# Moving weight buffers by 192 bytes: fourteen units to distance 0 from the activations, streamed weights to distance 192

## The chip, the cores and the metric

The kernel runs on one core of one Trainium2 chip. The metric is the device time of one execution in microseconds (us), lower is better. Five engines work side by side: TensorE (in the profile PE for matmuls, PEld for weight loads), VectorE (DVE), ScalarE (ACT), GpSimd (POOL) and SyncE (SP), which here only issues DMAs. A matmul takes two operands from the on-chip memory SBUF: the stationary one, called weights, is loaded by a weight load; the other is streamed past it. Results go to PSUM.

## What is computed

A trunk of two layers on 256 tokens of width 1024, in float32. Each layer is an FFN, a mixer, a second FFN and a gated input embedding, all residual:

```
for i in range(DEPTH):                                   # DEPTH = 2
    h = h + 0.5 * swiglu(rms_norm(h, ffn1_norm[i]), ffn1_w_gate[i], ffn1_w_up[i], ffn1_w_down[i])
    hn = rms_norm(h, mix_norm[i])
    if i % N_MIXERS == 0:  m = rglru_mixer(hn, ...)      # layer 0: recurrent mixer
    else:                  m = pool_mixer(hn, ...)       # layer 1: causal pooling
    h = h + m
    h = h + 0.5 * swiglu(rms_norm(h, ffn2_norm[i]), ffn2_w_gate[i], ffn2_w_up[i], ffn2_w_down[i])
    gate = jax.nn.sigmoid(rms_norm(h, ple_norm[i]) @ ple_w_gate[i])
    h = h + gate * (p[i] @ ple_w_proj[i])
return rms_norm(h, final_norm)

def swiglu(x, w_gate, w_up, w_down):
    return (jax.nn.silu(x @ w_gate) * (x @ w_up)) @ w_down
```

An FFN is 1024 wide outside and 2816 inside, so it holds most of the weights; there are four of them.

## The kernel before

All weights come as 328 units of 128x1024 floats, in the order in which they are used (`ORDER`). A unit is loaded by one DMA from SyncE into a `raw` tile, and then `split` makes of it a high part (a copy on ScalarE rounded to fp32r) and a low part (the rest, by a subtraction on VectorE), side by side in one `hl` tile of 2 x 1024 floats. Activations are split in the same way (`x`, `hid`, and `yr` with `ytp`). A product is then three fp32r matmuls (`mm3`): high weights with high activations, high weights with low activations, low weights with high activations. A unit feeds 24 such matmuls, of 128x128 weights and 256 streamed columns each. The units of the recurrent gates (`lru_gates`) are used unsplit, straight from `raw`. `unit` runs seven loads and four splits ahead of use.

Mostly the weights are stationary and activations stream. There are three exceptions: in `proj` (result `pp`) the transposed input embedding `ple_in`, which is one of the units, streams against the units `ple_proj`; in the pooling mixer the unit `pool_w` streams against activations (result `v`), and the units `pool_op` stream against `vhl` (result `po`).

The order of work in an FFN: the first two column pairs of gate and up are projected in two halves of the inner dimension (`project_all`), so that the work can begin before all of `x` is there. In the second half, `rstd_tokens` adds one-off matmuls for the sums of squares (`ss`, four of one column, each recorded as two) and `rstd_spread` two that spread the result over the partitions (`spread`, recorded as four). In three of the four FFNs, and in the RG-LRU layer, the spread falls in the middle of the second job of that half, and in the first FFN in the middle of the third. In the first gate projection it falls in the middle of the second job, in the last one in the middle of the first. Then the down projection of an earlier pair and gate and up of the next pair take turns up to pair 10 (results `acc`, `gate`, `up`), and nothing but these matmuls runs on TensorE. In the second FFN `proj` stands in the middle, ahead of pair 5.

Where the tiles lie follows from the pools, which are set up in this order:

```
rawp = ctx.enter_context(tc.tile_pool(name="raw", bufs=5))
hlp = ctx.enter_context(tc.tile_pool(name="hl", bufs=6))
gap = ctx.enter_context(tc.tile_pool(name="gap", bufs=1))     # one tile of 48 floats, 192 bytes
hp = ctx.enter_context(tc.tile_pool(name="h", bufs=6))
xp = ctx.enter_context(tc.tile_pool(name="x", bufs=7))
```

A `raw` tile takes 4096 bytes of each partition, an `hl` tile 8192, an `h` tile 2048, an `x` or `hid` tile 4096. Operands of matmuls begin at multiples of 512 bytes within their tile. Distance below means: start address of the streamed operand minus start address of the weights, in bytes modulo 512. The gap tile makes it 192 wherever activations stream against units; in `pp` it is 0, in `v` 320 (the gap counted the other way).

Of the kernel before, what the change touches and what calls it, by code (L numbers as in the profile page):

```python
# [10 lines left out]
F32R = mybir.dt.float32r  # L11
# [4 lines left out]
P = 128  # L16
# [12 lines left out]
U = 1024  # L29
# [17 lines left out]
APART = 48  # L47
# [24 lines left out]
def stream_order():  # L72

    order = []

    def halves(*keys):

        return [k + (kh,) for kh in range(2) for k in keys]

    def ffn(l, which, middle=()):  # L80
        def gu(p):
            return [(which, l, m, p, kh) for m in ("gate", "up") for kh in range(2)]

        def down(p):
            return [(which, l, "down", p, f) for f in range(2)]

        out = halves(*[(which, l, m, p) for p in range(2) for m in ("gate", "up")]) + down(0)
        for p in range(2, NF2):
            out += (list(middle) if p == NF2 // 2 else []) + gu(p) + down(p - 1)
        return out + down(NF2 - 1)  # L90

    def ple(l):
        return halves(*[("ple_gate", l, j) for j in range(NP_)])

    def proj(l):
        return [("ple_in", l)] + [("ple_proj", l, k) for k in range(2)]

    def pairs(kind, *ps):
        return [(kind, p, kh) for p in ps for kh in range(2)]

    def gates(hf):
        return [("lru_gates", hf, b) for b in range(-(-len(GATE_BLOCKS[hf]) // 8))]

    order += ffn(0, "ffn1")
    order += halves(*[(f"lru_{s[0]}", int(s[1])) for s in LRU_FIRST])
    for s in LRU_STEPS:
        kind, i = s[0], int(s[1])
        order += gates(i) if kind == "g" else pairs(f"lru_{kind}", i) if kind in "xb" else []
    order += [("lru_out", k) for k in range(NR)]
    order += ffn(0, "ffn2", proj(0)) + ple(0)  # L110
    order += ffn(1, "ffn1")
    order += [("pool_w", k) for k in range(2)] + proj(1) + [("pool_op", k) for k in range(2)]
    order += ffn(1, "ffn2") + ple(1)
    return order


ORDER = stream_order()


POOL_COLS = ((0, P + 16), (P, S))  # L120
# [3 lines left out]
def width(key):  # L124
    if key[0] == "lru_gates":
        return min(8, len(GATE_BLOCKS[key[1]]) - 8 * key[2]) * P
    if key[0] == "ple_in":
        return 2 * S
    if key[0] == "pool_op":
        return 4 * (POOL_COLS[key[1]][1] - POOL_COLS[key[1]][0])  # L130
    return U


def pack_units(a):
# [8 lines left out]
    for g, win in enumerate(WINDOWS):  # L143
        for t in range(S):
            lo = max(0, t + 1 - win)
            op[g, lo:t + 1, t] = np.float32(1.0) / np.float32(t + 1 - lo)
            op[g, t, t] = np.float32(1.0) / np.float32(t + 1 - lo) - np.float32(1.0)
    w = np.zeros((len(ORDER), P, U), np.float32)

    def rows(m):  # L150
        return m.reshape(-1, P, m.shape[1]).transpose(1, 0, 2).reshape(P, -1)

    for n, u in enumerate(ORDER):
        kind = u[0]
# [58 lines left out]
def trunk(ctx: ExitStack, tc: tile.TileContext, xT, vec, w, out):  # L213
# [4 lines left out]
    hlp = ctx.enter_context(tc.tile_pool(name="hl", bufs=6))  # L218
# [43 lines left out]
    def load(n, parts=1):  # L262
        whole = ORDER[n][0] == "lru_gates"
        raw = (box["gates"] if whole else rawp).tile([P, U], F32, tag="raw", name=f"raw{n}")
        step = width(ORDER[n]) // parts
        for i in range(parts):
            c = slice(i * step, (i + 1) * step)
            nc.sync.dma_start(raw[:, c], w[n, :, c])
        (units if whole else raws)[ORDER[n] if whole else n] = raw

    def split(n, parts=1):
        if n not in raws:
            return
        raw = raws.pop(n)
        hl = hlp.tile([P, 2, U], F32R, tag="hl", name=f"hl{n}")
        step = width(ORDER[n]) // parts
        for i in range(parts):
            c = slice(i * step, (i + 1) * step)
            nc.scalar.activation(hl[:, 0, c], raw[:, c], AF.Copy)  # L279
            nc.vector.tensor_tensor(hl[:, 1, c], raw[:, c], hl[:, 0, c].bitcast(F32), op=ALU.subtract)  # L280
        units[ORDER[n]] = hl

    def unit(*key):
        n = state["used"]
        assert ORDER[n] == key, (ORDER[n], key)
        for what, do, ahead in (("loaded", load, LOADS_AHEAD), ("split", split, SPLITS_AHEAD)):
            while state[what] < min(n + ahead + 1, len(ORDER)):
                do(state[what])
                state[what] += 1
        state["used"] = n + 1  # L290
        return units.pop(key)
# [546 lines left out]
    load_x(0)  # L838
    load(0, 2)
    split(0, 4)  # L840
    load_x(1)
    load(1, 2)
    split(1, 4)
    load(2)
    load(3)
# [39 lines left out]
```

## Time and profile before

| | |
|---|---|
| timed runs | 961.84, 961.54, 958.0 us; median 961.54 |
| profiled execution | 957.91 us, of which the span is 956.0 |
| granted TensorE clock, mean over the span | 0.994 |
| busy: TensorE, VectorE, ScalarE, GpSimd | 98%, 68%, 51%, 6% |
| read from memory | 171.37 MB, 180 GB/s over the span |

The share of TensorE's busy time says that a matmul is under way nearly always; a matmul's record lasts longer than its turn, since the next starts while it drains. How fast they follow each other is therefore read from the number of matmuls in a stretch, and not from the busy share. In the chain of waits, a piece is a run of instructions of one group that follow each other, with its start, its length and its count. Stages in the profile: first FFN up to 189 us, RG-LRU layer up to 298, second FFN up to 488, gate projection up to 512, third FFN up to 703, pooling up to 727, fourth FFN up to 915, gate projection and final norm up to the end.

### The profile page before, as it was taken

How to read it: one execution, taken by the hardware profiler on the slowest of the kernel's cores; microseconds unless marked ns; L12 is line 12 of the kernel's file. 1: busy time of each engine (PE TensorE's matmuls, PEld its weight loads, DVE VectorE, ACT ScalarE, POOL GpSimd, SP SyncE). 2: the span in 40 equal slices, each digit the busy share in tenths (PEclk: the TensorE clock that was granted, in tenths of full speed). 3: DMA queues.
4: the chain of work that ended last, by engine and by line, in shares of the span. 5: the costliest groups of instructions: out<-in, count | busy, mean ns of one | idle time of the engine just before them, and what ended most of it. 6: DMA issues, size and time to landing. Idle time of an engine off the chain costs nothing.

```text
span 956.0 us, 18714 instructions
## 1 busy us (share of the span) xinstructions
PE 937.9 (98%) x7888; PEld 929.7 (97%) x7888; DVE 651.4 (68%) x853; ACT 491.3 (51%) x634; POOL 55.6 (6%) x50
## 2 busy tenths in 40 slices
PE   9999999999999999999998999999989999999997
PEld 9999999999999999999998999999989999999996
DVE  7965565697797655665689755655579765556685
ACT  7544444558775444544457444444458544444443
POOL 1000000023201000000021000000011000000020
PEclk9999999999999999999999999999999999999999
DMA  8866666455445665665634665655534755656611
GB/s 300 288 218 203 195 197 196 159 176 182 133 155 163 210 185 165 219 208 178 207 120 169 218 197 179 193 184 179 184 110 131 250 195 170 205 178 187 188 45 45
DMA packets 49188, 173.63 MB, mean 182 GB/s; under 512 B 5584, under 2 KB 6224, under 8 KB 49104
## 3 DMA queue, kind: packets, MB, share of 16 engines
q1 hardware_dynamic: 48960, 172.29, 55.6%
q8 instruction: 61, 1.00, 0.4%
q14 instruction: 23, 0.19, 0.1%
q10 hardware_dynamic: 144, 0.15, 0.1%
HBM read 171.37 MB, written 1.05 MB: 180 GB/s over the span
## 4 chain that ended last, share of the span: by engine, by line
PE 64%; issue 21%; DVE 11%; ACT 3%; DMA 0%; POOL 0%; DVEq 0%; ACTq 0%; POOLq 0%
PE up0ffn L301 13%; PE gate0ffn L301 13%; PE acc0ffn L301 12%; PE up1ffn L301 6%; PE gate1ffn L301 6%; PE acc1ffn L301 6%; DVE hl L280 3%; DVE x L328 2%; PE x L301 2%; PE accl L301 1%; PE pp L301 1%; PE ri L301 1%; ACT hl L279 1%; PE xb L301 1%; DVE t L517 1%
## 5 line engine op out<-in xcount | busy, mean ns | idle before, releaser
L280 DVE TENSOR_TENSOR hl<-raw,hl 128x1024 fp32r<-128x1024 f32 (+1 forms) x326 | 385.2, 1199 | 228.1 <-ACT hl L279 228.0
L279 ACT ACTIVATE hl<-raw 128x1024 fp32r<-128x1024 f32 (+1 forms) x326 | 332.3, 1036 | 384.2 <-issue 93.0
L301 PE MATMUL gate1ffn<-x,hl 128*128 128x256 f32 x1056 | 130.1, 281 | 3.0 <-DVE x L328 2.4
L301 PEld LDWEIGHTS gate1ffn<-x,hl 128*128 128x128 f32 x1056 | 126.5, 189 | 4.0 <-DVE x L328 3.2
L301 PE MATMUL up1ffn<-x,hl 128*128 128x256 f32 x1056 | 129.5, 281 | 0.0
L301 PE MATMUL acc1ffn<-hid,hl 128*128 128x256 f32 x1056 | 127.6, 281 | 0.0
L301 PE MATMUL gate0ffn<-x,hl 128*128 128x256 f32 x1056 | 126.7, 278 | 0.2
L301 PEld LDWEIGHTS up1ffn<-x,hl 128*128 128x128 f32 x1056 | 126.4, 189 | 0.0
L301 PEld LDWEIGHTS acc1ffn<-hid,hl 128*128 128x128 f32 x1056 | 125.8, 189 | 0.0
L301 PE MATMUL up0ffn<-x,hl 128*128 128x256 f32 x1056 | 125.4, 277 | 0.0
L301 PE MATMUL acc0ffn<-hid,hl 128*128 128x256 f32 x1056 | 124.2, 277 | 0.0
L301 PEld LDWEIGHTS gate0ffn<-x,hl 128*128 128x128 f32 x1056 | 123.3, 188 | 0.8 <-DVE x L328 0.3
L301 PEld LDWEIGHTS up0ffn<-x,hl 128*128 128x128 f32 x1056 | 122.8, 188 | 0.0
L301 PEld LDWEIGHTS acc0ffn<-hid,hl 128*128 128x128 f32 x1056 | 122.1, 188 | 0.3 <-ACT hid L473 0.2
L341 POOL TENSOR_TENSOR sacc<-sq,sq 128x512 f32<-128x512 f32 x9 | 14.9, 1655 | 819.3 <-ACT sq L336 645.8
L328 DVE SCALAR_TENSOR_TENSOR x<-h,vt,x 128x256 fp32r<-128x256 f32 x64 | 48.6, 799 | 6.8 <-ACT x L327 6.8
L301 PE MATMUL ple<-x,hl 128*128 128x256 f32 x384 | 45.6, 278 | 0.2 <-DVE x L328 0.2
L301 PEld LDWEIGHTS ple<-x,hl 128*128 128x128 f32 x384 | 44.4, 188 | 0.5 <-DVE x L328 0.4
L473 ACT ACTIVATE hid<-gs 128x512 fp32r<-128x512 f32 x44 | 27.8, 633 | 17.0 <-DVE gs L471 17.0
L471 DVE TENSOR_TENSOR gs<-th,gs 128x512 f32<-128x512 f32 x44 | 30.4, 692 | 1.5
L327 ACT ACTIVATE x<-h,vt 128x256 fp32r<-128x256 f32 x64 | 28.5, 496 | 5.8 <-DMA vt<-vec 2.5
L474 DVE TENSOR_TENSOR hid<-gs,hid 128x512 fp32r<-128x512 f32 x44 | 30.1, 684 | 0.0
(134 smaller groups left out, 686.4 us busy)
## 6 DMA issues: line engine op xcount, KB each, us to landing
raw<-w SPq DMA_DIRECT2D x320, 512.0 KB, 4.2
raw<-w SPq DMA_DIRECT2D x7, 256.0 KB, 4.5
h<-xT SPq DMA_DIRECT2D x4, 256.0 KB, 6.1
out<-hg SPq DMA_DIRECT2D x3, 256.0 KB, 2.8
raw<-w SPq DMA_DIRECT2D x1, 288.0 KB, 2.6
raw<-w SPq DMA_DIRECT2D x2, 128.0 KB, 5.0
out<-hg SPq DMA_DIRECT2D x2, 128.0 KB, 2.0
vt<-vec ACTq DMA_DIRECT2D x1, 148.0 KB, 4.4
```

The lines of the kernel that those rows point to most:

```text
L279: nc.scalar.activation(hl[:, 0, c], raw[:, c], AF.Copy)
L280: nc.vector.tensor_tensor(hl[:, 1, c], raw[:, c], hl[:, 0, c].bitcast(F32), op=ALU.subtract)
L301: nc.tensor.matmul(o, lhsT, rhs, start=self.first, stop=self.left == 0, skip_group_check=True)
L327: nc.scalar.activation(xt[:, 0, c], h[:, c], AF.Copy, scale=g)
L328: nc.vector.scalar_tensor_tensor(xt[:, 1, c], h[:, c], g, xt[:, 0, c].bitcast(F32), op0=ALU.mult, op1=ALU.subtract)
L341: nc.gpsimd.tensor_tensor(acc, self.acc, sq, op=ALU.add)
L471: nc.vector.tensor_tensor(gs, th, gs, op=ALU.mult)
L473: nc.scalar.activation(hid[:, 0], gs, AF.Copy)
L474: nc.vector.tensor_tensor(hid[:, 1], gs, hid[:, 0].bitcast(F32), op=ALU.subtract)
L517: nc.vector.tensor_tensor(t, accs[j].ps, wide(rq), op=ALU.mult)
```

## The change

The `hl` tile gets 128 floats more (2176 floats, 8704 bytes, a multiple of 512), and a unit's parts begin at an offset in it: 48 floats (192 bytes) for the units in `LEVEL` and for `ple_in`, 96 floats for `pool_w`, 0 for all others. The units in `LEVEL` then stand at distance 0 to the activations; `pp` and `v` come to distance 192. In every FFN two units are in `LEVEL`: the first whole one after the spread (`gate` of pair 1, in the first FFN `up` of pair 1, second half), and the first half of `gate` of pair 6. The other six are in the RG-LRU layer (`lru_x` 2 and 3, `lru_b` 3, `lru_out` 1) and one in each gate projection. The order of instructions on every engine, and what each waits for, is as before.

```
+LEVEL = {(f"ffn{i}", l, "up" if (i, l) == (1, 0) else "gate", 1, 1) for i in (1, 2) for l in range(2)}
+LEVEL |= {(f"ffn{i}", l, "gate", 6, 0) for i in (1, 2) for l in range(2)}
+LEVEL |= {("lru_x", 2, 1), ("lru_x", 3, 0), ("lru_b", 3, 0), ("lru_out", 1), ("ple_gate", 0, 2, 1), ("ple_gate", 1, 1, 1)}
+assert LEVEL <= set(ORDER)
+
+OFFSET = {"ple_in": APART, "pool_w": 2 * APART}
...
         raw = raws.pop(n)
-        hl = hlp.tile([P, 2, U], F32R, tag="hl", name=f"hl{n}")
+        at = APART if ORDER[n] in LEVEL else OFFSET.get(ORDER[n][0], 0)
+        hl = hlp.tile([P, 2 * U + P], F32R, tag="hl", name=f"hl{n}")[:, at:at + 2 * U].rearrange("p (v u) -> p v u", v=2)
```

## Rows read from the trace of the kernel before

**Rows 1.** The page, busy us, share of the span, instructions.
```profile
PE 937.9 (98%) x7888; PEld 929.7 (97%) x7888; DVE 651.4 (68%) x853; ACT 491.3 (51%) x634; POOL 55.6 (6%) x50
```
**Rows 2.** Waits of TensorE: waited for, us in total, times, longest.
```profile
PE v L301 <- DVE x L328: 2.7, 4, 0.8
PE gate1ffn L301 <- DVE x L328: 2.4, 4, 0.8
PE spread L385 <- DVE dg L384: 1.7, 1, 1.7
PE accl L301 <- DVE ytp L700: 1.5, 1, 1.5
...
```
**Rows 3.** Chain of waits, second FFN, 366 to 400 us: start, length, piece.
```profile
373.44 5.65 PE acc0ffn L301 x48
379.09 5.76 PE pp L301 x48
384.85 5.47 PE gate0ffn L301 x48
390.32 5.44 PE up0ffn L301 x48
```
**Rows 4.** Windows: length, then busy (count) by engine, clock, DMA share, GB/s.
```profile
core 0: us, PE busy (x) PEld busy (x) DVE busy (x) ACT busy (x) POOL busy (x), PEclk, DMA share, GB/s
42.00:178.00 136.00, 136.00 (x1202) 136.00 (x1201) 84.85 (x99) 62.10 (x67) 0.00 (x0) 1.00 0.64 203
...
540.00:692.00 152.00, 152.00 (x1293) 152.00 (x1292) 88.46 (x90) 66.59 (x72) 0.00 (x0) 1.00 0.59 186
713.00:719.50 6.50, 6.50 (x32) 6.50 (x32) 4.01 (x15) 4.40 (x9) 0.00 (x0) 0.50 0.67 243
719.90:722.50 2.60, 2.60 (x24) 2.60 (x23) 2.49 (x4) 1.81 (x4) 0.00 (x0) 1.00 0.50 175
```
**Rows 5.** Chain of waits, first FFN, 18 to 46 us.
```profile
28.33 2.83 PE up0ffn L301 x24
...
40.02 2.49 PE gate0ffn L301 x22
```
**Rows 6.** Chain of waits, start of the second FFN, 282 to 322 us.
```profile
304.51 2.83 PE gate0ffn L301 x24
307.34 0.79 PE ss L348 x8
...
310.96 2.72 PE gate0ffn L301 x24
...
315.04 0.44 PE spread L385 x4
...
316.90 2.83 PE gate0ffn L301 x24
```
**Rows 7.** Chain of waits, start of the fourth FFN, 700 to 760 us.
```profile
744.66 0.45 PE spread L385 x4
...
746.52 2.83 PE gate1ffn L301 x24
```
**Rows 8.** Timeline of TensorE, 703 to 733 us: start, us, group, count.
```profile
727.05 0.80 PE L301 MATMUL pp<-hl,hl 128*128 128x256 f32 x5
```
**Rows 9.** Groups by line, 728.2 to 729.7 us: count, busy us, mean ns, idle before.
```profile
L301 PE MATMUL gate1ffn<-x,hl 128*128 128x256 f32 x16 | 2.0, 277 | 0.0
```
**Rows 10.** Groups by line, first FFN, 42 to 178 us.
```profile
L280 DVE TENSOR_TENSOR hl<-raw,hl 128x1024 fp32r<-128x1024 f32 x52 | 62.8, 1221 | 45.2 <-ACT hl L279 45.2
L279 ACT ACTIVATE hl<-raw 128x1024 fp32r<-128x1024 f32 x50 | 52.2, 1060 | 69.9 <-issue 21.4 <-PE acc0ffn L301 21.1 <-PE up0ffn L301 14.2
...
L301 PE MATMUL gate0ffn<-x,hl 128*128 128x256 f32 x389 | 45.6, 276 | 0.0
```
**Rows 11.** Groups by line, third FFN, 540 to 692 us.
```profile
L301 PE MATMUL gate1ffn<-x,hl 128*128 128x256 f32 x432 | 52.3, 281 | 0.0
```
**Rows 12.** Chain of waits, RG-LRU layer, 200 to 262 us.
```profile
224.66 5.67 PE xb L301 x48
...
230.95 1.48 DVE xc L688
```

## The prediction

> **What bounds the kernel now.** I read the busy times first. TensorE is busy 98% of the span, VectorE 68%, ScalarE 51% [rows 1]. Next, the waits of TensorE: the four longest entries, 2.7, 2.4, 1.7 and 1.5 us, belong to changes of stage and make 8.3 of 956 us [rows 2]. Inside the long FFN stretches there is no wait at all, and the DMA share there is 0.6 [rows 4]. So nothing feeds TensorE too slowly. What is left is the pace at which it takes its own matmuls. A change that moves addresses and no instruction can only matter there.
>
> So the pace must be read. In the chain of waits a piece is a run of matmuls with its length, so length over count is the time from one start to the next. Nearly all matmuls here have one shape (128x128 weights, 256 columns) and the same full clock, yet three paces appear [rows 3]: 48 matmuls of `acc0ffn` in 5.65 us (117.8 ns), 48 of `pp` in 5.76 us (120.0 ns), 48 of `up0ffn` in 5.44 us (113.3 ns). The windows show the same over long stretches [rows 4]. From 42 to 178 us there are 1202 matmuls in 136 us, from 540 to 692 us 1293 in 152 us, and from 752 to 904 us that row comes again. A window also counts the two or three that overlap its edges, which gives 113.3 against 117.8 ns, below called the short and the long pace. These are the same instructions with the same distance between operands, in different layers. So the pace is a mode: it holds for 150 us and more, and something else selects it.
>
> **What selects it.** Every weight tile is 8192 bytes and weight columns begin at multiples of 512 bytes. The 192-byte gap between the weights and all later tiles therefore puts streamed activations 192 bytes from the weights, modulo 512. Two kinds of matmul differ: `pp` streams a tile of the weights' own pool (distance 0), and `v` streams one against activations held as weights (320). Around them I read this:
> - The four one-off matmuls of the token sums and the two of the spread can flip the mode. In the second FFN the pace is 117.9 before the sums, 113.3 after them, and 117.9 again after the spread [rows 6]. Behind the spread it is long in the first and the last FFN too [rows 5, 7], and long it stays.
> - A stall can flip it to short. In the first FFN the pace goes from 24 matmuls in 2.83 us at 28 us to 22 in 2.49 us, 113.2 each, at 40 us [rows 5]; between them the first down projection has waited for its hidden tile.
> - The distance-0 stretch `pp` at 379 us is entered at the long pace, runs at 120.0 and leaves the short one behind: the next 48 take 5.47 us, then 5.44 [rows 3]. The second `pp`, at the end of the pooling stage, shows 120 again at full clock (24 records in 2.60 us, the edges counted) [rows 4]; its last five matmuls come just before `gate1ffn`, whose records right after have a mean of 277 ns [rows 8, 9]. The mean duration is 276 in the stretch of short pace in the first FFN [rows 10] and 281 over `gate1ffn` at the long one [rows 11].
> So two exits from distance 0 are on record, and both lead to the short pace.
>
> The Trainium skill speaks against this reading: "TensorE: Matmul & The Clock Gate", section "Step-by-step: what each phase is for", says that TensorE reads the streamed operand and the weights through two independent ports, so a weight load takes no read bandwidth from a running matmul. By that rule the distance would be worth nothing and the sum 0. The trace's 120.0 ns at distance 0 does not agree; it is the fourth rival below.
>
> **The change part by part.** No instruction, wait or queue entry moves; only addresses do. The new tile is 2176 x 4 = 8704 bytes, again a multiple of 512, so what lies behind it keeps its distance. Fourteen units of 24 matmuls go from 192 to 0, the two `pp` groups (48 each) from 0 to 192, `v` from 320 to 192. My model: a unit at distance 0 costs 24 x 120.0 = 2.88 us, against 2.72 at the short pace and 2.83 at the long one, and hands over the short one. Saved per matmul of long pace: 5.65 - 5.44 = 0.21 us for 48 [rows 3], 4.4 ns each.
> - First FFN, already at the short pace: the unit after the spread +0.05 us, the one at the seventh column pair +0.16. Sum +0.2.
> - RG-LRU layer: one unit at the short pace ahead of the gates, +0.16. Behind the gates `xb` is at the long one (48 in 5.67 us), but from 230 us the chain runs through VectorE and ends in a wait on `ytp` [rows 2, 12]; what TensorE gains or pays there is hidden by that. Sum +0.2.
> - Second FFN: long pace from the spread to `pp`, 504 matmuls (24 of `up`, then 10 groups of 48), -504 x 4.4 = -2.2. `pp` at 113.3: -48 x 6.7 = -0.32. The two units +0.05 and +0.16. Sum -2.3.
> - First gate projection: +0.16.
> - Third FFN: after the unit behind the spread stand 1416 matmuls, 24 of them in the second unit at distance 0. 1392 x 4.4 = -6.1, the two units +0.1. Sum -6.0.
> - Pooling: `v` waits for VectorE between its groups [rows 2], so 0. `pp` there: 24 at full clock, -0.16. Bounds: -0.3 to +0.3, its 48 times the whole spread of paces.
> - Fourth FFN: as the third, -6.0. Last gate projection +0.16.
> Total: +0.2 +0.2 -2.3 +0.16 -6.0 -0.16 -6.0 +0.16 = -13.7 us. The cover: in the window of short pace of the first FFN the splits take 1060 ns on ScalarE and 1221 ns on VectorE per unit [rows 10], against 2.72 us of matmuls, and these engines are busy 62.1 and 84.9 of 136 us with no wait of TensorE [rows 4]. So the shorter pace uncovers nothing. The split itself writes 192 bytes further on for the fourteen units; if each took twice its 1.2 us it would still fit into 2.7.
>
> The profiled execution took 957.91 us (956.0 in the span). That gives 944.2. The timed runs of before are 958.0, 961.54 and 961.84, so this execution lies 3.6 below the median. The trace has one stretch that could explain such a step. From 713 to 719.5 us the granted clock was 0.50, that is 1.2 instead of 2.4 GHz [rows 4], behind four waits of `v` [rows 2]; the 6.5 us of that window at half speed cost about 3.3. Whether the longer ones had a second such stretch, or the long pace where this one had the short, no row shows. In the second case the change removes the difference, in the first it stays. I take half of 3.6: **946.0 us**, with 940.9 (no half-clock stretch) and 947.8 at the sides.
>
> **Rivals.**
> 1. *One long FFN stretch does not flip.* `pp` was 48 long, a unit is 24, so a unit leaves at another point of its pattern. A stretch that stays at the long pace gives back 6.0: 952.0. For it: the mode hangs on small things [rows 6]. Against: the units behind the spreads are entered alike.
> 2. *Entered short, it exits long.* No row shows distance 0 entered from the short pace. Then the unit behind the spread makes the pace short and the one at the seventh pair spoils it, with 744 matmuls to come, 3.3 us. First FFN +3.3, second -2.2 +3.3 -0.3, third and fourth -2.9 each (648 matmuls), the units' own cost and gate projections at the long pace +1.6: -0.1. With half of 3.6 that is 959.6, no change.
> 3. *The other side: a unit of 24 always exits at the long pace.* It decides from the first FFN on: 744 matmuls there turn long, +3.3; in the second FFN `pp` no longer resets, so the 912 matmuls behind it stay long, +4.0; the units and the gate projections +1.2. Total +8.5, or 968.2. For it: the long pace stands behind every FFN spread [rows 5 to 7], so it is easy to fall into. Against: both exits on record went short.
> 4. *The distance does nothing,* and `pp` has its pace because of what it streams, and the flip at 385 us was chance. Then the change does not do what it says: 957.9 in this execution, 961.5 in the median. Against: `pp` shows 120.0 in both places.
>
> **Chances.** Forecast 0.72, rival 1 0.08, rival 2 0.07, rival 3 0.08, rival 4 0.05. What a measurement of this kernel can tell from no change is about 0.5%, 4.8 us. Faster: 0.72 + 0.08 = 0.80. Same: 0.07 + 0.05 = 0.12. Slower: 0.08. The forecast with its clock stretches covers 940 to 948; to hold 8 in 10 the range takes in rival 1 and a little above it, 940 to 956, and leaves out rivals 2 to 4.
>
> **What would show it.** In the profile after, the chain pieces of 48 in the third and fourth FFN should read 5.44 instead of 5.65, and the mean `gate1ffn` matmul 276 to 277 ns instead of 281. The fourteen units should run at 120.0, both `pp` groups at 113 to 118. No new entry should stand among TensorE's waits. I am wrong if a long stretch still reads 5.65 behind one of the units (rivals 1 to 3), or if the units run at the pace of their neighbours (rival 4).

## The result, and the profile after

The change makes the kernel slower by 0.8%: 965.69 us in the median (962.73 to 971.34, 6 runs) against 961.44 (958.0 to 966.69, 6 runs), ratio 1.0081 with a 95% interval of 1.0052 to 1.0110. The forecast was 946.0, with 940 to 956 as the range. The third rival, in which a unit always hands over the long pace, had 968.2.

The profiled execution of the kernel after took 965.23 us, against 957.91. Its page, part 1, answers to [rows 1]: the same share, a longer span of 963.4 us.

```profile
PE 947.1 (98%) x7888; PEld 938.9 (97%) x7888; DVE 651.6 (68%) x853; ACT 491.3 (51%) x634; POOL 55.4 (6%) x50
```

The waits of TensorE, answering to [rows 2], hold nothing new, and the wait on `ytp` is shorter (0.4 instead of 1.5 us). So the 7.4 us more are pace again.

```profile
PE v L310 <- DVE x L337: 2.7, 4, 0.8
...
PE accl L310 <- DVE ytp L709: 0.4, 1, 0.4
```

The windows of the kernel after, columns as in [rows 4], the first two in the first FFN, then the second (behind pair 6), the third and the fourth:

```profile
42.00:97.00 55.00, 55.00 (x488) 55.00 (x487) 36.23 (x49) 25.02 (x27) 0.00 (x0) 1.00 0.68 215
108.00:190.00 82.00, 82.00 (x699) 82.00 (x698) 47.56 (x51) 35.42 (x40) 0.00 (x0) 1.00 0.58 186
...
412.00:490.00 78.00, 78.00 (x665) 78.00 (x664) 44.94 (x46) 33.09 (x37) 0.00 (x0) 1.00 0.61 189
...
550.00:700.00 150.00, 150.00 (x1275) 150.00 (x1275) 86.00 (x88) 65.01 (x71) 0.00 (x0) 1.00 0.59 185
759.50:910.00 150.50, 150.50 (x1280) 150.50 (x1279) 87.74 (x90) 66.11 (x72) 0.00 (x0) 1.00 0.60 188
```

Without the edges these are 113.3 ns from one matmul to the next up to 97 us and 117.8 in the four others. The chain of waits shows the turn in the first FFN, where the first half of `gate` of pair 6 is a unit of the set (24 at 120.0 and 24 at 117.8 make the 5.70):

```profile
97.45 5.44 PE acc0ffn L310 x48
102.89 5.70 PE gate0ffn L310 x48
108.60 5.65 PE up0ffn L310 x48
```

In the second FFN it shows the unit behind the spread, entered at 1.42 us for 12 and left at 2.83 for 24; compare [rows 6].

```profile
318.65 0.45 PE spread L394 x4
319.09 1.42 PE up0ffn L310 x12
320.51 2.88 PE gate0ffn L310 x24
323.38 2.83 PE up0ffn L310 x24
```

And further on `pp`, now at distance 192, which resets nothing any more; compare [rows 3].

```profile
377.09 5.65 PE acc0ffn L310 x48
382.74 5.65 PE pp L310 x48
388.40 5.65 PE gate0ffn L310 x48
```

The sum of these: 744 matmuls of the first FFN turned long, at 4.4 ns 3.3 us; the 912 behind `pp` in the second, 4.0 us; together 7.3 of the 7.4 that the span grew. That this fits to 0.1 is in part luck: the execution after also ran 0.5 us late from its start (the first `up0ffn` group of pair 2 begins at 43.05 instead of 42.52 us), and small gains elsewhere, such as the shorter wait on `ytp`, made up for that. The third and fourth FFN were long before and are long now. The units themselves did run at 120.0.

### The profile page after: what moved, and what is told of

Same layout as the page of the kernel before. It is cut to its first block, busy times and chain, and to the rows that moved or that the text cites. A ratio compares the mean times of both kernels' runs of the same rounds, so it can differ in the third digit from the quotient of the medians.

```text
span 963.4 us, 18714 instructions
## 1 busy us (share of the span) xinstructions
PE 947.1 (98%) x7888; PEld 938.9 (97%) x7888; DVE 651.6 (68%) x853; ACT 491.3 (51%) x634; POOL 55.4 (6%) x50
## 4 chain that ended last, share of the span: by engine, by line
PE 69%; issue 20%; DVE 7%; ACT 2%; DMA 1%; POOL 0%; SPq 0%; DVEq 0%; ACTq 0%; POOLq 0%
PE up0ffn L310 13%; PE gate0ffn L310 13%; PE acc0ffn L310 12%; PE up1ffn L310 6%; PE gate1ffn L310 6%; PE acc1ffn L310 6%; PE gb L310 2%; PE ri L310 2%; DVE hl L289 2%; DVE x L337 2%; PE x L310 2%; PE accl L310 2%; PE pp L310 1%; PE xb L310 1%; ACT hl L288 1%
## 5 line engine op out<-in xcount | busy, mean ns | idle before, releaser
L310 PE MATMUL gate0ffn<-x,hl 128*128 128x256 f32 x1056 | 129.1, 280 | 0.4
L310 PE MATMUL up0ffn<-x,hl 128*128 128x256 f32 x1056 | 127.8, 280 | 0.0
L310 PE MATMUL acc0ffn<-hid,hl 128*128 128x256 f32 x1056 | 127.0, 280 | 0.0
L310 PEld LDWEIGHTS gate0ffn<-x,hl 128*128 128x128 f32 x1056 | 125.6, 189 | 1.3 <-ACT hl L288 0.4
L310 PEld LDWEIGHTS up0ffn<-x,hl 128*128 128x128 f32 x1056 | 125.2, 189 | 0.0
L310 PEld LDWEIGHTS acc0ffn<-hid,hl 128*128 128x128 f32 x1056 | 124.8, 189 | 0.3 <-ACT hid L482 0.2
```

What stands on the lines that cost most here:

```text
L310: nc.tensor.matmul(o, lhsT, rhs, start=self.first, stop=self.left == 0, skip_group_check=True)
```

## The experiments

Two questions were open: whether the units make the long pace at all, and why `pp` at distance 0 left the short one and the units leave the long one. A run of matmuls leaves, or hands over, the pace at which the matmuls behind it run, which stand at distance 192 again; it is entered at the pace of those ahead of it.

**Only the units.** The set as in the change, `pp` and `v` as before.

```
-OFFSET = {"ple_in": APART, "pool_w": 2 * APART}
+OFFSET = {}
```

> The fourteen units at distance 0, as in the change; the tiles that are streamed from the weights' pool stay where they were (pp at 0, v at 320). Theory A (a unit of 24 at distance 0 locks at an even 120 ns and hands over the long pace whatever it was entered at; pp's 48 are uneven, 117 to 124, and hand over the short one): the first FFN turns long at its seventh pair as in the change (+3.3 us against before), the second FFN turns short behind pp at about 385 us and long again at its seventh pair 150 matmuls later, so 0.6 us less than the change there; about 964.5 us by the profile, against 965.2 of the change and 957.9 of before. Rival B (it was not the units but the moved pp and v, or the larger tile): the first FFN stays short to its end, 113.3 ns from 42 to 178 us, and the time is that of before, 958 to 962.

965.76 us (964.81 to 967.29, 5 runs), ratio to before 1.006 (1.0040 to 1.0079). Its profiled execution took 967.2; the first FFN was long already from 35 us on, 594 matmuls or 2.6 us ahead of the unit at pair 6, and without that it stands at 964.6, as expected. The second FFN shows both kinds of distance 0 within 30 us (chain of waits):

```profile
386.02 5.75 PE pp L310 x48
391.77 5.46 PE gate0ffn L310 x48
397.23 5.44 PE up0ffn L310 x48
...
408.11 5.70 PE gate0ffn L310 x48
413.81 5.65 PE up0ffn L310 x48
```

`pp` turns long into short, the unit of the set turns short into long. Rival B falls for the second FFN.

**Only what is streamed.** The set empty, `ple_in` and `pool_w` moved.

```
-LEVEL = {...}
+LEVEL = set()
```

> No unit at distance 0; ple_in moves by 192 bytes and pool_w by 384, so pp and v stand at distance 192. Theory A: the first FFN stays short throughout as before; pp runs at 117.8 in the second FFN and resets nothing, so that FFN stays long to its end: 912 matmuls x 4.4 ns = +4.0 us, less 0.1 for pp; about 961.8 by the profile. Rival B (moving pp and v, or the larger tile, is what costs): the first FFN turns long too and the time is near the change, 965.

965.81 us (959.4 to 969.78, 10 runs), ratio 1.004 (1.0007 to 1.0073). By the median alone this is rival B's 965. `pp` ran at 117.8 and the second FFN stayed long to its end, as expected: windows of TensorE (length, busy, count, clock, DMA share, GB/s), the first FFN and then the second behind `pp`.

```profile
54.00:184.00 130.00, 130.00 (x1106) 1.00 0.58 188
...
395.00:490.00 95.00, 95.00 (x809) 1.00 0.59 194
```

But the first FFN was long here too (117.8 in the first row), with no unit in it. From 35 us on that is 1362 matmuls, 6.0 us; the profiled 967.6 less 6.0 is 961.6, near the expected 961.8. The moved tiles are not the reason: the run with only the units, where they stay, came out long from 35 us on as well, and the change, where they move, short up to its unit at pair 6, with the same addresses up to there.

The timed runs show the same choice. Runs of one kernel with the same mean granted clock fall into two groups. The runs of before that were timed beside the experiments took, at 0.998, 954.9 to 956.0 us in five runs and 961.0 to 961.4 in three; at 0.994, 957.3 to 958.1 in seven and 963.1 to 963.8 in five. This kernel, at 0.998, took 959.4 and 965.2. The step is as large as the 6 us of the first FFN, and the profiled executions fit: before, with a short first FFN, is in the lower group (957.9 at 0.994), this one in the upper (967.6 at 0.993, where another run took 962.2). The lower run at 0.998 lies 3.4 to 4.5 us above the lower group of before, where 3.9 were expected. So rival B falls, and the pace of the first FFN is not set by the addresses: as far as these profiles show, it is chosen by chance between 33 and 40 us, where the first down projection begins and, in the profile before, its weight load waits 0.2 us for a hidden tile.

**Runs of other lengths.** Fifteen runs of 24, 48, 72, 96 and 144 at distance 0 (the recorded text says 240; the longest in this kernel is 144), by a set of unit names, `NEAR`, in place of the fourteen.

```
+def offset(key):
+    return APART if key in NEAR else 0
...
+        at = offset(ORDER[n])
```

> Probe, before's layout with larger tiles, and runs of 24, 48, 72, 96 and 240 matmuls at distance 0 at chosen places of the four FFNs (gate and up against x, once the down units against hid); pp at 0 as before. Length theory (a unit is too short, 48 is enough): runs of 48 and 96 leave 113.3 ns behind, runs of 24 leave 117.8. Pattern theory (what counts is whether the run locks at an even 120 or stays uneven as pp did, not how long it is): every even run leaves 117.8 whatever its length, and only an uneven one leaves 113.3.

967.89 us (one run). Every run left 117.8 behind, whatever its length; the chain of waits in the first FFN shows 24 (at 53.64), 48 (at 87.61) and 96 (at 155.72):

```profile
53.64 5.70 PE gate0ffn L320 x48
59.35 5.65 PE up0ffn L320 x48
...
87.61 5.76 PE gate0ffn L320 x48
93.37 5.65 PE up0ffn L320 x48
...
155.72 5.76 PE gate0ffn L320 x48
161.48 5.76 PE up0ffn L320 x48
167.24 5.65 PE acc0ffn L320 x48
```

The length theory falls. The pattern theory falls as well. In the profile of before the 48 of `pp` are uneven, single matmuls 280 to 287 ns; in the run with only the units they are even but for the first few, like the units, and still `pp` left the short pace. By tile (min/median/max ns), that run:

```profile
L310 PE MATMUL pp<-hl,hl x44: 278/283/283, 386.0 to 391.1; 128*128 128x256 f32 x44
```

**All distances.** The units of gate and up of each pair begin 16 bytes further on than those of the pair before it, from 0 to 496 bytes, and those of the last four pairs at 0, 192, 96 and 288 bytes.

```
+def offset(key):
+    if key[0] in ("ffn1", "ffn2") and key[2] in ("gate", "up") and key[3] >= 2:
+        return 4 * STEPS[SLOTS.index((key[0], key[1], key[3]))]
+    return 0
```

> Probe, before's layout with larger tiles; gate and up of each pair from the third on (96 matmuls each, 36 pairs in the four FFNs) begin at 0, 16, 32 ... 496 bytes in their tiles (then 0, 192, 96, 288 again), so their distance to the activations runs through 192, 176, 160 ... 208; the down units between them stay at 192. If weight loads and streamed reads meet in SBUF by address, the pace depends on the distance: 120.0 at 0, 113.3 or 117.8 at 192, other values elsewhere, and neighbouring distances of 16 bytes agree in groups of the size of whatever they share. If they do not meet (independent ports), all 36 pairs run at 113.3 or 117.8.

965.44 us (one run). The pace does follow the distance, but not in groups, and what it is depends on the pace before as well: 113.3 at 192 entered short; 116.7 at 48 and 32; 117.3 to 120.2 elsewhere. At 160 it was 120.0 in the pairs entered short and 117.3 in the one entered long. Distances 256 apart agree where they were entered alike, so distances are given modulo 256 from here on. What the 48 `acc` matmuls behind each pair run at, which all stand at 192, is the more useful reading: long behind 0, 80, 224 and 240, each time it was tried; short behind 16, 32, 48, 64, 96, 112, 128, 144, 160, 176 and 208. From the chain of waits, distance 160, 96 and 32, then 0, 496 (240; only its `acc`) and 448 (192), each with what follows (the last `up` of the pair, then `acc`):

```profile
76.36 5.76 PE up0ffn L312 x48
82.12 5.45 PE acc0ffn L312 x48
...
144.11 5.75 PE up0ffn L312 x48
149.86 5.44 PE acc0ffn L312 x48
...
355.17 5.60 PE up0ffn L312 x48
360.76 5.44 PE acc0ffn L312 x48
...
394.40 5.76 PE up0ffn L312 x48
400.15 5.65 PE acc0ffn L312 x48
...
417.17 5.65 PE acc0ffn L312 x48
...
462.03 5.44 PE up0ffn L312 x48
467.47 5.44 PE acc0ffn L312 x48
```

Distance 160 and distance 0 cost the same 5.76 us and hand over different paces. So the fourteen units are a selector, and the change put it on a wrong setting. How many there are is not shown: pairs at 0 and 80 turned the short pace long, those at 224 and 240 were only tried behind the long pace and may just have kept it. Likewise a turn from long to short was seen at 16, 48, 64, 96, 160 and 208 only; the others were only tried behind the short pace.

**Distance 48 for the same fourteen units.**

```
-        at = APART if ORDER[n] in LEVEL else OFFSET.get(ORDER[n][0], 0)
+        at = 36 if ORDER[n] in LEVEL else OFFSET.get(ORDER[n][0], 0)
```

> The change with one number altered: the fourteen units begin 144 bytes into their tiles (36 floats), at distance 48, where the probe of distances ran at 116.7 ns and left 113.3 behind from either pace. Theory A (a unit selects the pace that follows by its distance: 0 hands over the long one, 48 the short one): all four FFNs run at 113.3 behind their units; against the change the first gains 744 x 4.4 ns = 3.3 us, the second 6.3 (with pp), the third and fourth 6.1 each, the units themselves 1.1: about 942 us by the profile, and runs that differ less among themselves. Rival B (24 matmuls are too few, in the probe there were 96): the long pace stays behind the units, about 964. Rival C (the long pace comes by chance, whatever the units do): some stretches short and some long, 950 to 962.

944.45 us (942.85 to 949.21, 6 runs), ratio to before 0.9857 (0.9822 to 0.9893). Behind every unit of the FFNs the pace is short; the second FFN at its spread (chain), then the third FFN (window of TensorE, 1281 in 145 us, 113.3 each):

```profile
316.54 0.45 PE spread L394 x4
316.99 1.42 PE up0ffn L310 x12
318.40 2.80 PE gate0ffn L310 x24
321.21 2.72 PE up0ffn L310 x24
```

```profile
545.00:690.00 145.00, 145.00 (x1281) 1.00 0.60 191
```

Theory A holds, and 24 matmuls are enough. One number, the offset of fourteen units, is worth 21 us between this and the change (by the ratios to before, 0.9857 and 1.0081).

**Distance 96.** The same edit with 24 floats.

> The change with the units at distance 96 (96 bytes into their tiles). There the probe ran at 120.0 ns as at distance 0, and yet left 113.3 behind, so it differs from the change in nothing but the pace that is handed over. Theory A: 943 us by the profile, 1 us over the run at distance 48 for the units' own pace. Rival D (what costs is the units' own 120 ns, and the pace behind them is not theirs): no better than the change, 964.

951.25 us (944.5 to 956.49, 8 runs), ratio 0.9916 (0.9880 to 0.9952): better than the change, so rival D falls, but not the 943 expected, and the runs spread over 12 us. In the profiled execution the second and third FFN are short, the first from its unit at pair 6 on, and the fourth is long behind both of its units (windows of TensorE, second and fourth FFN):

```profile
326.00:374.00 48.00, 48.00 (x426) 1.00 0.59 191
...
752.00:900.00 148.00, 148.00 (x1259) 1.00 0.59 187
```

Behind the four spreads the unit's own 24 took 2.87 or 2.88 us, 120 ns each, whichever pace they left. What differs is the stretch ahead of the spread: 24 matmuls took 2.72 us there in the first and fourth FFN, where the unit left the long pace, and 2.82 to 2.83 in the second and third, where it left the short one. These are four cases of one execution. The units at pair 6 do not follow a rule of that kind: in the first and in the fourth FFN they were entered long, and left the short pace in the first, the long one in the fourth. So distance alone does not decide at 96, and what else does stays open. The probe, with runs of 96, had not shown that.

**Distance 0 from the other side.** A gap of 256 bytes, all units 64 bytes in, those of the set at 0.

```
-        at = APART if ORDER[n] in LEVEL else OFFSET.get(ORDER[n][0], 0)
+        at = 0 if ORDER[n] in LEVEL else 16
...
-    apart = gap.tile([P, APART], F32, name="apart")
+    apart = gap.tile([P, 64], F32, name="apart")
```

> The same fourteen units at distance 0, but by the other side: the gap is 256 bytes, all units begin 64 bytes into their tiles (distance 192), those of the set at 0 bytes (distance 256, which is 0 modulo 256), and pp is at distance 0 as in before. Theory A2 (the distance alone decides, and distances 256 apart are alike): units at 120.0 and the long pace behind each of them. Rival E (where the weights themselves stand decides: in pp they stood where all units stand, and it handed over the short pace): the units hand over the short pace and the FFNs run at 113.3.

963.14 us (one run). The units hand over the long pace as in the change, `pp` the short one as in before (chain of waits, with the unit at 405.31); rival E falls.

```profile
383.22 5.75 PE pp L310 x48
388.97 5.46 PE gate0ffn L310 x48
...
405.31 5.70 PE gate0ffn L310 x48
```

**Fewer units at distance 48.** Eleven instead of fourteen: one in each FFN instead of two, but in the first FFN a second one at pair 3, behind the wait near 33 us, and `lru_out` 6 instead of 1.

```
+LEVEL = {(w, l, "gate", 1, 1) for w in ("ffn1", "ffn2") for l in range(2)} - {("ffn1", 0, "gate", 1, 1)}
+LEVEL |= {("ffn1", 0, "up", 1, 1), ("ffn1", 0, "gate", 3, 0)}
+LEVEL |= {("lru_x", 2, 1), ("lru_x", 3, 0), ("lru_b", 3, 0), ("lru_out", 6), ("ple_gate", 0, 2, 1), ("ple_gate", 1, 1, 1)}
...
+        at = 36 if ORDER[n] in LEVEL else OFFSET.get(ORDER[n][0], 0)
```

> Distance 48 as before, and one unit in each FFN instead of two (the one behind the spread; in the first FFN another at the fourth pair, behind the wait for the first hidden tile), and lru_out 6 instead of 1, behind the wait for ytp. Theory A: the second unit at the seventh pair does nothing where the pace is short already, so this is as fast as the run at distance 48 or 0.3 us faster (3 units less at 3.4 ns x 24, and 70 matmuls at the end of the RG-LRU layer at the short pace). If the pace can turn long by itself in the middle of an FFN, it is slower by up to 3.3 us for each.

943.56 us (942.31 to 946.05, 6 runs), ratio 0.9846 (0.9810 to 0.9882), 0.9 us under the run with fourteen, which these runs cannot tell apart. No long stretch stands in its profile behind a unit, so the pace does not turn by itself within an FFN. The runs lie within 3.7 us; those of before, on the same chip, within 8.8 (954.94 to 963.77, 15 runs). There are no two groups any more: the six times follow the mean granted clock, from 942.3 us at 0.996 to 946.1 at 0.991.

**Both operands of `pp` moved.** The set empty; `pp` at distance 0 by moving `ple_in` and `ple_proj`.

```
+LEVEL = set()
+OFFSET = {"ple_in": APART, "ple_proj": APART, "pool_w": 2 * APART}
```

> No unit of the set is moved. pp stands at distance 0 again, but now because both of its operands begin 192 bytes in (ple_in and ple_proj), so that at both of its ends it is the weights that jump, as in the units of the change, where in before it was the streamed tile. pool_w as in the change. Theory F (at distance 0 what jumps at the end of the run decides): pp's 48 hand over the long pace, 117.8 in gate behind it, and the second FFN stays long to its end. Rival G (pp differs from the units in what it streams, not in what jumps): pp hands over 113.3 as in before. Rival H (chance): either.

970.94 us (one run). The first FFN was long here by chance, as with only the streamed tiles moved, and the mean granted clock was 0.990, so the time says little. `pp` now leaves the long pace (chain of waits), so rival G falls:

```profile
379.13 5.66 PE acc0ffn L307 x48
384.78 5.75 PE pp L307 x48
390.54 5.65 PE gate0ffn L307 x48
```

This rests on one stretch of one execution. Against chance (rival H) stand the four exits of `pp` with the streamed tile moved (before, only the units, lengths, the other side), all short.

**Units behind the sums as well.** The run with fewer units and four more.

```
+LEVEL |= {("ffn1", 0, "gate", 0, 1), ("ffn2", 0, "up", 1, 0), ("ffn1", 1, "up", 1, 0), ("ffn2", 1, "up", 1, 0)}
```

> The run with fewer units at distance 48, and four units more at that distance: the first whole one behind the token sums of each FFN, where 36 to 48 matmuls ran at 117.8 up to the spread. Theory A: 36 x 4.4 ns in each of four FFNs, and 24 at 116.7 instead of 117.8: 0.7 us less, 942 to 943 us, which these runs can hardly tell from the run with fewer units (943.6).

943.36 us (943.08 to 944.23, 4 runs), ratio 0.9826 (0.9781 to 0.9871). Not to be told from the run with fewer units, as said. But the profile does not show what was expected of it: three of the four added units, which stand directly behind the sums, left the long pace. In the second FFN (chain of waits):

```profile
309.58 2.92 PE up0ffn L311 x24
312.50 2.83 PE gate0ffn L311 x24
```

Only the one in the fourth FFN, with 12 matmuls between it and the sums, left the short pace (2.80 us, then 2.72). So distance 48 does not select it from everywhere. All three kernels with units at distance 48 beat both kernels, before and the change.

## Why the prediction was wrong, point by point

- **What bounds the kernel.** Right. The paces moved the time by 22 us between kernels of the same instructions (965.2 for the change and 942.8 with fewer units at distance 48, both profiled at a mean granted clock of 0.994). The one wait that these profiles add, at the first `gate0ffn` group, is 0.3 to 1.3 us, and the one of 942.8 has 1.0 of it.
- **Two paces, held over long stretches, chosen at their start.** Right for distance 192, and shown: 113.3 and 117.8 in every profile. Other distances have other paces, such as 116.7 at 48.
- **"A unit at distance 0 ... hands over the short one."** This step failed. All units at distance 0 in the FFNs, in the change and in four experiments, handed over the long pace, 117.8, whether they were entered short or long and whatever their length. The two exits on record were both of `pp`, and in `pp` the streamed tile jumps to distance 0 and back, where in the units the weights jump. With that turned round in `pp`, it left the long pace too (one run). No position by itself fits: in the run from the other side weights at 0 with activations at 256 left the long pace, in before weights at 0 with a streamed tile at 0 the short one. The rows could have warned me: `pp` and the units agreed in distance, but not in which operand brings it about, and I took one for the other.
- **The terms.** First FFN +0.2 expected, +3.3 by its second unit; second -2.3 expected, +4.0, since `pp` at 192 resets nothing; third and fourth -6.0 each expected, 0. The terms of the third rival were these, with 968.2 against 965.7 measured; its +8.5 was 7.4 by the profiles.
- **"Short pace in the first FFN" as a property of before.** Wrong. As far as is seen it is chance: without any unit in it, it came out long in the profile with only the streamed tiles moved, and the timed runs of before fall into two groups 6 us apart at one granted clock. The clock counts beside it: within the lower group the time goes from 955 us at 0.998 to 961 at 0.990. So the 3.6 us between the profiled execution and the median, which I split in halves between clock and pace, were nothing to be halved: each run has its own clock and its own pace in the first FFN. The profiled execution, 957.9 at 0.994, belongs to the lower group.
- **The second rival** (entered short, it exits long) was right on the unit at pair 6 and wrong on the one behind the spread.
- **The fourth rival** (the distance does nothing) falls: with equal work, 36 pairs ran at 113.3 to 120.2 by their distance and by how they were entered. The Trainium skill, "TensorE: Matmul & The Clock Gate", section "Step-by-step: what each phase is for", has a weight load take no read bandwidth from the running matmul. The paces of these pairs do not agree with that, unless something other than the two reads makes the distance count; no run here separates that.

What stays open is what makes the distance count, and why a jump of the weights at distance 0 ends in another pace than a jump of the streamed tile. That distance 48 selects the short pace behind the FFN spreads is shown in three kernels; why it does, and why not directly behind the sums, is not.

## What to carry to other kernels

Where TensorE is busy all the time, read the time from one matmul to the next by stretch: a stretch can run 4% longer (117.8 against 113.3 ns) in a mode that no wait shows. Here the pace followed the distance between the start addresses of weights and streamed tile modulo 256 bytes, and a run of 24 matmuls at another distance could select the pace of what followed. Try all distances in one probe, and read what each leaves behind, not its own cost; then try the chosen one in its place, since 96 did well in the probe and not there. And before an effect is carried from one place to another, ask what else was different there: here it was which operand moved.

## What the runs showed of the hardware that was not expected

- The pace of a stretch depends on how it was entered, and holds for 150 us and more: 113.3 or 117.8 ns at one distance.
- Distances 256 bytes apart behave alike when entered alike: 0 and 256 in the run from the other side, 192 and 448 in the probe.
- Distance 160 and distance 0 both cost 120.0 ns a matmul when entered short, and leave 113.3 and 117.8 behind.
- The same addresses gave both paces in the first FFN, chosen between 33 and 40 us, and a step of 6 us between runs of one kernel at one granted clock.
- A run of 24 matmuls at distance 48 takes 2.80 us, against 2.72 at the short pace, and selected the short pace behind each FFN spread in three kernels; the kernel with eleven such units takes 0.985 of the time before.
